# Product-key experts: activations of key rows 48 to 111 made between the gates, and kept in DRAM until they are used

## The chip, the cores and the metric

The program runs on one core of a Trainium2 chip. The core has five engines with queues of their own: TensorE (PE, the matmuls), VectorE (DVE), ScalarE (ACT), GpSimd (POOL) and SyncE (SP, which here only issues DMAs). Each takes its instructions strictly in the order of its queue; semaphores order work between them. The metric is the time of one run on the device in microseconds (us), as the median of three runs.

## The reference

The program computes three transformer layers for 256 tokens with 1024 channels. The change touches the last step alone, a feed-forward layer of 128 x 128 = 16384 experts that are found by product keys:

```
q = (xc @ peer_wq)                     # 8 heads, two half queries each
s = einsum(q, peer_keys)               # scores against 2 x 128 keys
sv, si = top_k(s, 16)                  # best 16 of each half
top_s, pos = top_k(sum of all pairs, 16)
gate = softmax(top_s)                  # 16 experts for each head and token
act = gelu(einsum(peer_u[eidx], xc))
out = einsum(gate * act, peer_v[eidx])
```

Expert (i, c) has the first key i, from here on called its key row (0 to 127), and the second key c (0 to 127).

## The kernel before

The kernel computes the layer densely: gelu(u h) for all 16384 experts, times a gate that is zero wherever an expert was not chosen, times v. Everything stands with 128 partitions (the second key c) by 256 tokens for each key row. The function `peer` has three stages, and the function `peer_route` runs beside the first.

1. **Routing and the first activations.** For each of 8 heads `peer_route` makes the queries and scores on PE, and the best 16 on DVE, then yields; after each yield `peer` makes the activations of two pairs of key rows (`up`, L1939 to L1947). `up` for one pair loads two blocks of u of 512 KB (`wpair`, L448), splits each in two halves of 128x512 into a high part (a cast on ACT, L439) and a low part (a subtraction, L440), runs 2 x 8 x 3 = 48 matmuls (L415 to L417), and takes the gelu on ACT (L1947). In this stage the subtractions go to POOL. Rows 0 to 63 (32 pairs) are made here and stay in SBUF in `act`. The end of the routing turns the chosen keys and gates into `idx`, one transpose for each 128 tokens (`rt`, L2083, L2084).
2. **Gates.** The 64 groups of four tokens each get a gate matrix. `hots` makes one-hot matrices from `idx`: five of each six groups by one comparison on DVE (L1969) and four scalings on ACT (L1977), the sixth by eight comparisons on POOL (L1974, L1975), issued ahead of the other five. `gate` multiplies them on PE (L1983; each of the four products counts as two matmuls in the profile) into one PSUM bank `G` of four. Then DVE multiplies the bank's part for rows 0 to 63 into `act` (L1987), and ACT copies rows 64 to 119 to `Gate` (L1988) and rows 120 to 127 over `x` (L1989).
3. **Second product.** For each pair of rows, `gated` gives the gated activations, split into high and low, and 2 x 8 x 3 = 48 matmuls add v's product into four PSUM banks `acc`. For rows 64 to 127 `gated` first calls `up`, now with the subtractions on DVE, and multiplies by the gate (L2006). The weights of u and v share three load buffers and four split buffers (`weights5`, `weights5h`). At the end DVE adds the residual (L2020) and SP stores it (L2021).

The order of the instructions on each engine is fixed when the program is built: a scheduler moves instructions of different stages past each other where the dependences and buffers allow it (four of the 64 gate products stand among the last activations of stage 1, for one). The chip then runs each queue as it stands.

Of the kernel before, what the change touches and what calls it, by code (L numbers as in the profile page):

```python
# [8 lines left out]
F32, F32R = mybir.dt.float32, mybir.dt.float32r  # L9
# [5 lines left out]
PSUM, DRAM = bass.MemoryType.PSUM, bass.MemoryType.DRAM  # L15

T = 256
D = 1024
KT = 8
# [217 lines left out]
class Ring:  # L237
# [5 lines left out]
    def next(self, shape):  # L243
        self.i += 1
        p = self.pairs[self.i % len(self.pairs)]
        return Pair(*(t.rearrange("p (a b) -> p a b", b=shape[-1]) for t in (p.hi, p.lo)))


class K:
# [1673 lines left out]
    def peer(self):  # L1923

        nc, tc, A, mod = self.nc, self.tc, self.A, self.mod
        v_ = nc.vector
        m2 = mod[:, 96:144]
        sc = self.modscale("norm2_g_2", m2[:, 32:40], "sc6")
        HF = 64
        with ExitStack() as c:  # L1930
            p = c.enter_context(tc.tile_pool(name="pe", bufs=1))
            self.banks(c, a=4, u=2, r=2)

            xd = c.enter_context(tc.tile_pool(name="xwait", bufs=1, space=DRAM)).tile([128, KT, T], F32, name="xd")
            h = self.pair(p, [128, KT, T], "h6")
            self.scaled(self.x, self.r2, sc, m2[:, 24:32], h)
            idx = p.tile([128, 3, T], F32, name="idx")
            iota = p.tile([128, 128], F32, name="iota")
            act = p.tile([128, HF, T], F32, name="acts")  # L1939

            def up(i, out, eng=None):

                self.bank = "u"
                ps = self.psum("act")
                for j in range(2):
                    self.wT(ps[:, T * j:T * j + T], self.wpair(A["u"][i + j], eng), h)
                nc.scalar.activation(out, ps.rearrange("p (j t) -> p j t", j=2), AF.Gelu_apprx_tanh)  # L1947

            with ExitStack() as c2:
                self.W = c2.enter_context(tc.tile_pool(name="weights4", bufs=4))  # L1950
                self.Wh = c2.enter_context(tc.tile_pool(name="weights4h", bufs=8))
                for hd in self.peer_route(c2, h, idx, iota, xd):
                    for i in range(4 * hd, 4 * hd + 4, 2):
                        up(i, act[:, i:i + 2], nc.gpsimd)
                for i in range(32, HF, 2):
                    up(i, act[:, i:i + 2], nc.gpsimd)
            gp = c.enter_context(tc.tile_pool(name="peg", bufs=1))

            G = [gp.tile([128, 120 - HF, T], F32, name="Gate"), self.x]
            self.W = c.enter_context(tc.tile_pool(name="weights5", bufs=3))  # L1960
            self.Wh = c.enter_context(tc.tile_pool(name="weights5h", bufs=4))
            with ExitStack() as c2:
                tp = c2.enter_context(tc.tile_pool(name="pet", bufs=3))
                self.bank = "a"

                def hots(t4, pool):
                    o = tp.tile([128, 2, 4, 128], F32, tag="op" if pool else "o", name=f"oh{t4}", bufs=2 if pool else 3)
                    if not pool:
                        v_.tensor_tensor(o, iota.rearrange("p (a b i) -> p a b i", a=1, b=1).to_broadcast([128, 2, 4, 128]),  # L1969
                                         idx[:, 0:2, 4 * t4:4 * t4 + 4].rearrange("p a (t o) -> p a t o", o=1).to_broadcast([128, 2, 4, 128]), op=OP.is_equal)  # L1970
                    for t in range(4):
                        i1, i2, w = (idx[:, n, 4 * t4 + t:4 * t4 + t + 1] for n in range(3))
                        if pool:
                            nc.gpsimd.tensor_scalar(o[:, 0, t], iota, i1, w, op0=OP.is_equal, op1=OP.mult)  # L1974
                            nc.gpsimd.tensor_scalar(o[:, 1, t], iota, i2, None, op0=OP.is_equal)  # L1975
                        else:
                            nc.scalar.activation(o[:, 0, t], o[:, 0, t], AF.Copy, scale=w)  # L1977
                    return o

                def gate(t4, o):  # L1980
                    ps = self.psum("G")
                    for t in range(4):
                        nc.tensor.matmul(ps[:, 128 * t:128 * t + 128], o[:, 1, t], o[:, 0, t], start=True, stop=True)  # L1983
                    pv = ps.rearrange("p (t i) -> p t i", t=4)
                    ts = slice(4 * t4, 4 * t4 + 4)
                    av = act[:, :, ts].rearrange("p i t -> p t i")
                    v_.tensor_mul(av, av, pv[:, :, :HF])  # L1987
                    nc.scalar.copy(G[0][:, :, ts].rearrange("p i t -> p t i"), pv[:, :, HF:120])  # L1988
                    nc.scalar.copy(G[1][:, :, ts].rearrange("p i t -> p t i"), pv[:, :, 120:])  # L1989

                for g0 in range(0, T // 4, 6):
                    ahead = hots(g0, True)
                    for t4 in range(g0 + 1, min(g0 + 6, T // 4)):
                        gate(t4, hots(t4, False))
                    gate(g0, ahead)
            tp = c.enter_context(tc.tile_pool(name="pea", bufs=2))
            self.bank = "a"
            acc = [self.psum("acc") for _ in range(4)]

            def gated(i):  # L2000
                if i < HF:
                    a = act[:, i:i + 2]
                else:
                    a = tp.tile([128, 2, T], F32, tag="a", name=f"a{i}")
                    up(i, a)
                    v_.tensor_mul(a, a, G[0][:, i - HF:i - HF + 2] if i < 120 else G[1][:, i - 120:i - 118])  # L2006
                return self.split(a, self.pair(tp, [128, 2, T], f"ap{i}", ("ah", "al")))

            nxt = gated(0)
            for i in range(0, 128, 2):  # L2010
                a, nxt = nxt, gated(i + 2) if i < 126 else None
                for j in range(2):
                    vs = self.wpair(A["v"][i + j].rearrange("p (a d) -> p a d", a=2))
                    for m in range(KT):
                        self.mm(acc[m // 2][:, T * (m % 2):T * (m % 2) + T], vs[:, m // 4, 128 * (m % 4):128 * (m % 4) + 128], a[:, j],
                                i + j == 0 and m % 2 == 0, i + j == 127, skip_group_check=True)
            xr = act[:, 0:KT]
            nc.sync.dma_start(xr, xd)
            for m in range(KT):
                v_.scalar_tensor_tensor(xr[:, m], acc[m // 2][:, T * (m % 2):T * (m % 2) + T], m2[:, 40 + m:41 + m], xr[:, m], op0=OP.mult, op1=OP.add)  # L2020
                nc.sync.dma_start(self.out[:, m], xr[:, m])  # L2021
# [133 lines left out]
```

## Time and profile before

| | us |
|---|---|
| runs | 3642.47, 3640.02, 3639.27 (median 3640.02) |
| profiled execution | 3639.1 |
| its span on the core | 3637.3 |
| the last layer's feed-forward, from its first matmuls to the end | about 2711 to 3637.3 |
| gates, from the first product of the dense stretch to the first matmul of the second product | 2977.2 to 3078.8 |

The profile is of one execution. A span is counted from its start, and the start times of instructions count from there too. "Busy" for an engine is the time in which an instruction of its own was being executed; consecutive instructions overlap, so the distance from start to start says how long one occupies the engine, and its duration says when the next engine may go on. The mean granted clock of TensorE over the span was 0.929 of full speed. The median of the runs is 0.9 above the profiled execution, and that is 1.8 above its span.

### The profile page before, as it was taken

To read this page: it belongs to the slowest core of one execution; us is meant where nothing else is said; L and a number is where in the kernel's file an instruction comes from. 1 tells how busy PE (TensorE), PEld (TensorE's weight loads), DVE (VectorE), ACT (ScalarE), POOL (GpSimd) and SP (SyncE) were. 2 spreads that over 40 slices of the span, in tenths; PEclk is the share of its full clock that TensorE was granted. 3 is DMA by queue.
4 is the path that set the end of the run, shared out by engine and by line. 5 is a ranking of instruction groups with operands and counts; after the bars stand their busy time and mean duration, and the time that the engine had idled before them with its cause. 6 is when DMAs were issued, how large, how long until landed. Compare 5 with 4: busy or idle time off the path is not lost.

```text
span 3637.3 us, 69980 instructions
## 1 busy us (share of the span) xinstructions
PE 3312.3 (91%) x27824; PEld 2815.9 (77%) x27824; DVE 2323.3 (64%) x4465; ACT 1691.4 (47%) x3082; POOL 795.0 (22%) x789
## 2 busy tenths in 40 slices
PE   6989889989999999967898989899989887999999
PEld 4769767866678888555777767777879887999999
DVE  3568857754369999367556675666367838555555
ACT  4445332433246666134334344434346568555554
POOL 0000312200000000033232233323338978000000
PEclk9999987989999999978688999889789999999999
DMA  7656573387988999931011111101545330555555
GB/s 286 245 213 225 199 266 101 114 324 320 367 339 339 342 334 339 361 106 39 25 42 37 34 54 44 36 32 58 154 150 178 120 128 18 193 185 182 184 183 165
DMA packets 155276, 641.87 MB, mean 176 GB/s; under 512 B 17192, under 2 KB 36280, under 8 KB 111040
## 3 DMA queue, kind: packets, MB, share of 16 engines
q1 hardware_dynamic: 140736, 563.94, 43.5%
q0 software_dynamic: 14208, 73.41, 5.6%
q8 instruction: 220, 3.60, 0.4%
q14 instruction: 112, 0.92, 0.1%
HBM read 625.87 MB, written 11.40 MB: 175 GB/s over the span
## 4 chain that ended last, share of the span: by engine, by line
PE 40%; DVE 9%; POOL 3%; ACT 2%; issue 1%; DMA 1%; POOLq 0%; SPq 0%; DVEq 0%; ACTq 0%
PE acc L415 3%; PE acc L416 3%; PE acc L417 3%; PE act L417 3%; PE act L415 3%; PE act L416 3%; POOL oh L1974 1%; POOL oh L1975 1%; DVE rs L361 1%; DVE G L1802 1%; PE mc L1682 1%; PE U L1738 1%; PE S L1754 1%; PE R L1732 1%; PE R L1728 1%
## 5 line engine op out<-in xcount | busy, mean ns | idle before, releaser
L1719 POOL MEMSET UV<- 64x256 f32 x64 | 19.5, 306 | 1024.3 <-DVE xT L1169 817.7
L422 PE MATMUL mg<-mg,xs 128*64 128x256 f32 x1408 | 185.0, 386 | 3.7 <-ACT xf L1095 3.7
L1242 ACT ACTIVATE msg<-mg 128x128 f32<-128x128 f32 (+1 forms) x154 | 42.3, 274 | 260.0 <-PE mg L422 190.7
L422 PEld LDWEIGHTS mg<-mg,xs 128*64 128x64 f32 x1408 | 106.2, 138 | 68.1 <-issue 15.8
L361 DVE RECIPROCAL rs<-rs 128x256 f32<-128x256 f32 (+1 forms) x48 | 112.6, 2347 | 53.6 <-ACT rs L360 53.6
L330 PE MATMUL mod<-wm,c 128*32 128x256 f32 x1152 | 98.7, 447 | 51.8 <-DMA wm<-mods 47.3
L327 POOL DMA_DIRECT2D wm<-mods x64 | 34.9, 545 | 390.0 <-PE mod L330 373.4
L330 PEld LDWEIGHTS mod<-wm,c 128*32 128x32 f32 x1152 | 37.5, 121 | 89.3 <-DMA wm<-mods 47.5
L1983 PE MATMUL G<-oh 128*128 128x128 f32 x512 | 80.9, 317 | 25.4 <-ACT oh L1977 12.8
L1983 PEld LDWEIGHTS G<-oh 128*128 128x128 f32 x512 | 74.0, 215 | 31.9 <-ACT oh L1977 17.5
L1243 DVE TENSOR_TENSOR msg<-msg,mg 128x128 f32<-128x128 f32 (+1 forms) x154 | 43.4, 282 | 76.4 <-ACT msg L1242 76.0
L1738 PE MATMUL U<-R,TT 64*64 64x64 f32 x512 | 51.0, 247 | 39.1 <-DVE R L1733 30.9
L1969 DVE TENSOR_TENSOR oh<-iota,idx 128x1024 f32<-128x1024 f32 x53 | 76.1, 1440 | 10.0 <-PE G L1983 10.0
L1987 DVE TENSOR_TENSOR acts<-acts,G 128x256 f32<-128x256 f32 x64 | 44.8, 716 | 58.9 <-ACT acts L1947 49.8
L1738 PEld LDWEIGHTS U<-R,TT 64*64 64x64 f32 x512 | 40.7, 154 | 51.2 <-DVE R L1733 34.2
L1977 ACT ACTIVATE oh<-oh,idx 128x128 f32<-128x128 f32 x212 | 68.1, 392 | 14.2 <-DVE oh L1969 13.9
L1739 ACT ACTIVATE UV<-U 64x256 f32<-64x256 f32 x64 | 24.1, 377 | 102.4 <-PE U L1738 102.2
L1761 DVE TENSOR_TENSOR S<-S,S 128x256 f32<-128x256 f32 x48 | 20.3, 422 | 76.5 <-PE S L1754 76.2
L1974 POOL TENSOR_SCALAR oh<-iota,idx 128x128 f32<-128x128 f32 x44 | 63.6, 1444 | 12.5 <-PE G L1983 12.5
L1146 DVE COPY mgt<-mg 128x128 f32<-128x128 f32 x44 | 12.8, 290 | 74.7 <-PE mg L1139 74.4
L1733 DVE COPY R<-R 64x256 f32<-64x256 f32 x64 | 26.5, 413 | 51.3 <-PE R L1732 50.7
L1802 DVE TENSOR_TENSOR G<-G,X 128x1 f32<-128x1 f32 (+14 forms) x120 | 57.1, 476 | 3.3
(11874 smaller groups left out, 13577.6 us busy)
## 6 DMA issues: line engine op xcount, KB each, us to landing
mg<-m_gu SPq DMA_DIRECT2D x176, 1024.0 KB, 7.5
md<-m_dn SPq DMA_DIRECT2D x88, 1024.0 KB, 7.7
wm<-mods POOLq DMA_DIRECT2D x64, 1024.0 KB, 5.7
w<-u SPq DMA_DIRECT2D x128, 512.0 KB, 3.4
w<-v SPq DMA_DIRECT2D x128, 512.0 KB, 3.3
w<-w_in SPq DMA_DIRECT2D x132, 256.0 KB, 2.6
w<-e_gu SPq DMA_DIRECT2D x44, 512.0 KB, 4.4
w<-e_in SPq DMA_DIRECT2D x24, 512.0 KB, 4.2
```

The lines of the kernel that those rows point to most:

```text
L330: nc.tensor.matmul(ps[32 * j:32 * j + 32, :256], c[:, 2 * kp + k, :], ws[:, 2 * j + k, :], start=kp + k == 0, stop=kp + k == 4)
L361: nc.vector.reciprocal(t[:, :n], t[:, :n])
L415: mm(ps, w.hi, h.hi, start=start, stop=False, **kw)
L416: mm(ps, w.hi, h.lo, start=False, stop=False, **kw)
L417: mm(ps, w.lo, h.hi, start=False, stop=stop, **kw)
L422: mm(ps, w, h, start=start, stop=stop, **kw)
L1738: nc.tensor.matmul(ps[:64, c0_:c0_ + 64], TT[hb, d, o, c], R[hb, d, o], start=True, stop=True)
L1802: v_.tensor_mul(pr[:, :t, :t], G[:, t:t + 1, :t].to_broadcast([128, t, t]), X[:, :t, :t].rearrange("p u s -> p s u"))
L1969: v_.tensor_tensor(o, iota.rearrange("p (a b i) -> p a b i", a=1, b=1).to_broadcast([128, 2, 4, 128]), idx[:, 0:2, 4 * t4:4 * t4 + 4].rear ...
L1974: nc.gpsimd.tensor_scalar(o[:, 0, t], iota, i1, w, op0=OP.is_equal, op1=OP.mult)
L1977: nc.scalar.activation(o[:, 0, t], o[:, 0, t], AF.Copy, scale=w)
L1983: nc.tensor.matmul(ps[:, 128 * t:128 * t + 128], o[:, 1, t], o[:, 0, t], start=True, stop=True)
```

## The change

The rows that are made ahead of the gates are cut from 64 to 48. Rows 48 to 111 (32 pairs) are made in the gates' stage, one `up` after each second gate, with the subtractions on DVE; their gelu goes to a buffer of its own (`as`, two of them), and SP stores it to DRAM (`ad`, 256 KB a pair). In the second product these 32 pairs are loaded back into `a` (three buffers in place of two) ahead of their multiplication by the gate. Rows 112 to 127 (8 pairs) are made there as before. `Gate` grows from 56 to 72 rows, `act` shrinks from 64 to 48, and POOL's one-hot buffer is one in place of two.

```diff
-        HF = 64
+        HF, HD = 48, 112
...
+            ad = [dr.tile([128, 2, T], F32, name=f"ad{i}") for i in range(HF, HD, 2)]
...
-                    o = tp.tile([128, 2, 4, 128], F32, tag="op" if pool else "o", name=f"oh{t4}", bufs=2 if pool else 3)
+                    o = tp.tile([128, 2, 4, 128], F32, tag="op" if pool else "o", name=f"oh{t4}", bufs=1 if pool else 3)
...
                 def gate(t4, o):
+                    self.bank = "a"
                     ps = self.psum("G")
...
+                def spill(i):
+                    a = tp.tile([128, 2, T], F32, tag="as", name=f"as{i}", bufs=2)
+                    up(i, a)
+                    nc.sync.dma_start(ad[(i - HF) // 2], a)
+
+                rows = iter(range(HF, HD, 2))
+                n = 0
                 for g0 in range(0, T // 4, 6):
                     ahead = hots(g0, True)
-                    for t4 in range(g0 + 1, min(g0 + 6, T // 4)):
-                        gate(t4, hots(t4, False))
-                    gate(g0, ahead)
+                    for t4 in (*range(g0 + 1, min(g0 + 6, T // 4)), g0):
+                        gate(t4, ahead if t4 == g0 else hots(t4, False))
+                        n += 1
+                        if n * (HD - HF) // 2 // (T // 4) > (n - 1) * (HD - HF) // 2 // (T // 4):
+                            spill(next(rows))
...
                 else:
-                    a = tp.tile([128, 2, T], F32, tag="a", name=f"a{i}")
-                    up(i, a)
+                    a = tp.tile([128, 2, T], F32, tag="a", name=f"a{i}", bufs=3)
+                    if i < HD:
+                        nc.sync.dma_start(a, ad[(i - HF) // 2])
+                    else:
+                        up(i, a)
                     v_.tensor_mul(a, a, G[0][:, i - HF:i - HF + 2] if i < 120 else G[1][:, i - 120:i - 118])
```

How the queues change is shown at three places. First, POOL's queue where the routing ends, before the change (`w...l` is the low part of a block of u, `oh` a one-hot matrix):

```order
L440 TENSOR_TENSOR w26660l<-w_30176,w26660h 128x512
...
L1974 TENSOR_SCALAR oh_30962<-iota,idx 128x128
L1975 TENSOR_SCALAR oh_30962<-iota,idx 128x128
L1974 TENSOR_SCALAR oh_31049<-iota,idx 128x128
L1975 TENSOR_SCALAR oh_31049<-iota,idx 128x128
L1974 TENSOR_SCALAR oh_31049<-iota,idx 128x128
L1975 TENSOR_SCALAR oh_31049<-iota,idx 128x128
L440 TENSOR_TENSOR w26664l<-w_30176,w26664h 128x512
L1974 TENSOR_SCALAR oh_31049<-iota,idx 128x128
L1975 TENSOR_SCALAR oh_31049<-iota,idx 128x128
L440 TENSOR_TENSOR w26670l<-w_30210,w26670h 128x512
```

and the same place after it:

```order
L440 TENSOR_TENSOR w26660l<-w_30208,w26660h 128x512
...
L1977 TENSOR_SCALAR oh_30434<-iota,idx 128x128
L1978 TENSOR_SCALAR oh_30434<-iota,idx 128x128
L440 TENSOR_TENSOR w26664l<-w_30208,w26664h 128x512
L440 TENSOR_TENSOR w26670l<-w_30242,w26670h 128x512
L440 TENSOR_TENSOR w26674l<-w_30242,w26674h 128x512
L440 TENSOR_TENSOR w26690l<-w_30278,w26690h 128x512
```

With one one-hot buffer in place of two, 8 comparisons stand ahead of w26664l where 12 stood, and none between the subtractions that follow.

Second, ACT's queue amid the gates, before:

```order
L1988 COPY Gate<-G_31353 128x4x56
L1989 COPY xT<-G_31353 128x4x8
L1977 ACTIVATE oh_31406<-oh_31406,idx 128x128 x4
L1988 COPY Gate<-G_31367 128x4x56
L1989 COPY xT<-G_31367 128x4x8
L1977 ACTIVATE oh_31420<-oh_31420,idx 128x128 x4
```

and after, one cycle of two gates and one pair of rows (`as` is the pair's gelu, `w...h` the casts of the next pair's weights):

```order
L1950 ACTIVATE as_30665<-act_30666 128x512
L1992 COPY Gate<-G_30752 128x4x72
L1993 COPY xT<-G_30752 128x4x8
L1980 ACTIVATE oh_30860<-oh_30860,idx 128x128 x4
L439 CAST w26970h<-w_30876 128x512
L1992 COPY Gate<-G_30766 128x4x72
L1993 COPY xT<-G_30766 128x4x8
L1980 ACTIVATE oh_30946<-oh_30946,idx 128x128 x2
L439 CAST w26974h<-w_30876 128x512
L1980 ACTIVATE oh_30946<-oh_30946,idx 128x128 x2
L439 CAST w26980h<-w_30910 128x512
```

A fourth cast and the next gelu follow. On PE each two gates' products now stand between the 48 matmuls of one pair and those of the next, where before the products stood one behind the other.

Third, SP's queue in the second product, where before only loads of v and u stood, after the change (`a` is a pair of activations that comes back from `ad`):

```order
L456 DMA w_35492<-v 128x1024
L2019 DMA a_35560<-ad_27466 128x512
L456 DMA w_35526<-v 128x1024
L456 DMA w_35567<-v 128x1024
L2019 DMA a_35635<-ad_27467 128x512
L456 DMA w_35601<-v 128x1024
L456 DMA w_35642<-v 128x1024
```

One load of 256 KB stands ahead of each two of 512 KB. In the gates' stage the stores to `ad` stand in the same way, one behind each two loads of u.

## Rows read from the trace of the kernel before

**Rows 1.** Busy time by stage: stretch, length, PE, PEld, DVE, ACT, POOL; PEclk, DMA share, GB/s.
```profile
2713.00:2859.00 146.00, 146.00 (x1223) 145.97 (x1222) 109.45 (x510) 99.47 (x192) 125.50 (x99) 1.00 0.55 180
2859.00:2926.00 67.00, 48.38 (x366) 47.19 (x364) 54.85 (x26) 29.88 (x67) 61.48 (x40) 0.90 0.31 107
...
2977.20:3078.80 101.60, 76.49 (x481) 69.96 (x481) 91.41 (x109) 90.88 (x312) 95.85 (x72) 0.90 0.00 1
3078.80:3631.95 553.15, 553.15 (x4608) 552.96 (x4608) 322.71 (x481) 285.53 (x475) 0.00 (x0) 1.00 0.55 181
```
**Rows 2.** The chain that ended last, from 2700 on, by line.
```profile
by line: PE acc L415 13.1%; PE acc L416 13.1%; PE acc L417 13.0%; PE act L417 11.5%; PE act L415 11.5%; PE act L416 11.5%; POOL oh L1974 5.8%; POOL oh L1975 4.9%; DVE oh L1969 1.7%; PE q L416 1.5%; PE q L417 1.5%; PE q L415 1.4%; issue 1.1%
```
**Rows 3.** Waits from 2855 to 3080: total us, times, longest.
```profile
DVE acts L1987 <- ACT acts L1947: 49.8, 1, 49.8
...
PE G L1983 <- POOL oh L1975: 10.5, 7, 2.4
```
**Rows 4.** Timeline of PE: start, us, engine, line, op, names, idle before and its releaser.
```profile
2905.31 0.58 PE L417 MATMUL act<-h6h,w26664l 128*128 128x256 f32 x1 [10.10 <-POOL w26664l L440]
...
2922.71 0.28 PE L416 MATMUL act<-h6l,w26734h 128*128 128x256 f32 x1
2926.01 0.39 PE L415 MATMUL act<-h6h,w26750h 128*128 128x256 f32 x1 [3.02 <-ACT w26750h L439]
...
3004.25 3.12 PE L1983 MATMUL G<-oh 128*128 128x128 f32 x24 [0.37 <-ACT oh L1977]
```
**Rows 5.** Timeline of POOL, ahead of w26664l and amid the gates.
```profile
2899.98 0.60 POOL L1975 TENSOR_SCALAR oh<-iota,idx 128x128 f32<-128x128 f32 x1
...
2904.00 1.26 POOL L440 TENSOR_TENSOR w26664l<-w,w26664h 128x512 fp32r<-128x512 f32 x1
...
3005.97 1.98 POOL L1974 TENSOR_SCALAR oh<-iota,idx 128x128 f32<-128x128 f32 x1
```
**Rows 6.** Timeline of DVE, amid the gates and where POOL subtracts.
```profile
2912.75 8.82 DVE L1969 TENSOR_TENSOR oh<-iota,idx 128x1024 f32<-128x1024 f32 x1 [9.97 <-PE G L1983]
...
2923.43 0.69 DVE L440 TENSOR_TENSOR w27660l<-w,w27660h 128x512 fp32r<-128x512 f32 x1 [1.86 <-ACT w27660h L439]
2924.04 0.69 DVE L440 TENSOR_TENSOR w27661l<-w,w27661h 128x512 fp32r<-128x512 f32 x1
...
3001.91 0.73 DVE L1987 TENSOR_TENSOR acts<-acts,G 128x256 f32<-128x256 f32 x1
3002.52 1.25 DVE L1969 TENSOR_TENSOR oh<-iota,idx 128x1024 f32<-128x1024 f32 x1
3003.65 0.73 DVE L1987 TENSOR_TENSOR acts<-acts,G 128x256 f32<-128x256 f32 x1
```
**Rows 7.** Timeline of ACT, in stage 1 and amid the gates.
```profile
2924.34 0.62 ACT L439 CAST w27671h<-w 128x512 fp32r<-128x512 f32 x1
2924.86 0.59 ACT L1947 ACTIVATE acts<-act 128x512 f32<-128x512 f32 x1
2925.35 0.61 ACT L439 CAST w26750h<-w 128x512 fp32r<-128x512 f32 x1
...
3002.06 1.28 ACT L1977 ACTIVATE oh<-oh,idx 128x128 f32<-128x128 f32 x4
3003.25 0.53 ACT L1988 COPY Gate<-G 128x224 f32<-128x224 f32 x1
3003.58 0.26 ACT L1989 COPY xT<-G 128x32 f32<-128x32 f32 x1
```
**Rows 8.** Timeline where the second product starts.
```profile
3078.76 0.51 PE L415 MATMUL acc<-ap0h,w27660h 128*128 128x256 f32 x2 [1.85 <-ACT ap0h L439]
```
**Rows 9.** DMA issues from 3100 to 3600, and the densest DMA stretch near, as Rows 1.
```profile
w<-v SPq DMA_DIRECT2D x112, 512.0 KB, 3.3
w<-u SPq DMA_DIRECT2D x62, 512.0 KB, 4.0
...
2930.00:2934.00 4.00, 4.00 (x33) 4.00 (x33) 0.00 (x0) 0.79 (x2) 3.55 (x3) 0.91 0.98 368
```

More of the change, by code (lines that the diff above doesn't have):

```diff
@@ L1932, in peer @@
             self.banks(c, a=4, u=2, r=2)
-            xd = c.enter_context(tc.tile_pool(name="xwait", bufs=1, space=DRAM)).tile([128, KT, T], F32, name="xd")
+            dr = c.enter_context(tc.tile_pool(name="xwait", bufs=1, space=DRAM))
+            xd = dr.tile([128, KT, T], F32, name="xd")
+            ad = [dr.tile([128, 2, T], F32, name=f"ad{i}") for i in range(HF, HD, 2)]
             h = self.pair(p, [128, KT, T], "h6")
```

## The prediction

> **What bounds the kernel now.** I read the busy time by stage first. In the second product PE is busy for all of 553.15 us, at full clock, with 4608 matmuls, 0.1200 us each [rows 1]; DVE and ACT are busy for 58% and 52% there. So this stage lasts as long as its matmuls, and taking a pair of rows out of it takes 48 x 0.1200 = 5.76 us off it. In the gates' stretch (2977.2 to 3078.8) PE is busy for 76.49 of 101.60 us at a clock of 0.90, and DMA carries nothing. The chain that ended last says who holds PE up there: POOL's one-hot comparisons (5.8% + 4.9%) stand on it [rows 2], with DVE and ACT close behind, each about 90% busy. How little of that stretch PE needs is read from its timeline: 24 gate matmuls in a row take 3.12 us with a last one of 0.28, so (3.12 - 0.28) / 23 = 0.123 each, and the 480 of this stretch 59 us [rows 1, 4].
>
> The waits name the third fact: DVE's first multiplication of gates waited 49.8 us for the last gelu of stage 1 [rows 3]. The routing was over by then; the gates stood behind the activations of rows 48 to 63, which came at PE's pace. Before that, PE itself lost 10.10 us to one weight part, w26664l, which POOL made only after twelve comparisons, and 3.02 us to ACT [rows 4, 5].
>
> **What is removed, added and moved.** The number of matmuls stays. 8 pairs leave stage 1 and 24 leave the second product; these 32 go between the gates. What the change can win is PE's idle time and slow clock, no more.
>
> *Stage 1.* Up to the wait for w26664l all queues are the same. POOL now makes 8 comparisons ahead of it, the last of which ended at 2899.98 + 0.60 = 2900.6, so the part comes 3.4 us sooner than at 2904.0 and PE resumes at 2901.9 in place of 2905.31 [rows 4, 5]. From there before went through the last part that both have (w26734): 2922.71, and 10 matmuls more, that is 18.7 us, with one gate's 8 matmuls (1.0 us) among them that now come later: 17.7 us, so the first gate starts at 2901.9 + 17.7 = 2919.6. The 3.02 us wait after it [rows 4] stood at a place where ACT had one-hot scalings to wait for; in the new order it has none, and I count it as gone.
>
> *Gates.* One cycle of two gates and one pair is 16 x 0.123 + 48 x 0.120 = 7.73 us of PE; 32 cycles are 247.4 us. Can the others keep that pace? Occupied time, from start to start: a cast 0.52, a gelu 0.49, four scalings 1.19, the copy to Gate 0.33 for 224 elements and up to 0.42 for 288, the small copy 0.26 [rows 7]; a subtraction 0.61, a comparison 1.13, the multiplication 0.61 for 256 elements, between 0.46 and 0.61 for 192 (I take 0.5) [rows 6]. 53 of the 64 gates use ACT and DVE for their one-hots, 11 use POOL. ACT has 4 x 0.52 + 0.49 + 53/32 x 1.19 + 2 x 0.66 = 5.9 us a cycle, DVE 4 x 0.61 + 2 x 0.5 + 53/32 x 1.13 = 5.3. Both are under 7.73, but each waits for the other, so the loop counts: cast 0.62 to its end, subtraction 0.61, multiplication 0.5, comparison 1.25 to its end, four scalings 1.19, cast 0.52, two copies 0.66, two scalings 0.6, cast 0.52, two scalings 0.6, cast 0.52: 7.6 us. That holds for the 21 cycles with two ACT gates. With one from POOL the loop is 0.62 + 0.61 + 0.5 + 1.25 + 1.19 + 0.66 + 2 x 0.52 = 5.9. The mean is 7.0, and since one-hots and parts are made a cycle ahead of PE, the mean decides: PE sets the pace, with 32 x 0.73 = 23 us to spare. I put 4 us for single waits; the bounds are 0 and what the rivals below take. POOL has 8 comparisons every three cycles (23 us); at the slowest seen, 1.98 each, they take 16 [rows 5], so that one buffer does where two were.
>
> *DMA.* Each cycle loads 1 MB and stores 256 KB, about 170 GB/s; the second product then reads 1.25 MB for 5.76 us of PE, 228 GB/s. Both lie well below the 368 GB/s of one stretch of stage 1 [rows 9]. A store waits in SP's queue for its gelu, with the next loads of u behind it; these are for two cycles later and land in 3.3 to 4.0 us [rows 9], so nothing is late. In the second product the load of a pair waits for a subtraction two pairs back, with loads of v behind it. Three buffers at 2.88 us a row give a round of 8.6 us; a landing of 4.0 and the two splits (1.2 to 2.9) leave 1.7 or more. So 0 there, and at worst the price given below.
>
> *Second product.* It begins behind the last pair's gelu: gelu, cast of ap0 and hand-over are about what PE waited there before, 1.85 us [rows 8]. Then 128 x 24 + 16 x 24 = 3456 matmuls at 0.1200: 414.9 us. From the last matmul's end (3631.95, the end of that stretch) to the end of the span 5.35 us as before.
>
> *Sum.* 2919.6 + 247.4 + 1.85 + 414.9 + 5.35 = 3589.1, and 4 for waits: 3593 of span, against 3637.3. With the 1.8 around the span 3595, against 3639.1 of the same execution; the median of the runs shown is 0.9 above that, within what I can't resolve. **I predict 3595 us, 1.2% faster.** The gain is made of the 42 us of the gates' stretch that PE did not need, the 3.4 + 3.0 us at the end of stage 1, and slow clock behind its waits, less the 4 us of waits and what the cycles' start costs.
>
> **Rivals.**
> 1. *The loop through ACT and DVE sets the pace.* For it: it is only 0.13 us shorter than PE's cycle where both gates are ACT's. If four hand-overs cost 0.3 us more each, the cycles are 8.8 and 7.1, mean 8.2: 32 x 0.5 = 16 us, 3607. Against: waits of PE on ACT amid the gates come from one-hots that had no lead, and now they have a cycle's.
> 2. *POOL and DVE block each other.* For it: a comparison on POOL took 1.98 beside DVE's, against 0.60 for the shorter kind alone [rows 5], and one comparison on DVE took 8.82 while POOL subtracted without a pause, against 1.25 [rows 6]. If each of the 88 POOL comparisons holds DVE up for 0.7 us, that is 1.9 a cycle: 7.0 + 1.9 - 7.73 = 1.2 over, 38 us, 3629. Against: amid the gates DVE's comparisons took 1.25 each beside a POOL that never paused; POOL was the one that waited.
> 3. *Slower, by the same place.* If POOL, once ahead, keeps DVE out for its whole batch of eight, as for that one comparison (8.82 - 1.25 = 7.6 us), the eleven batches cost 83 us, less the 23 to spare: 60 over, 3651. It turns into a loss from some 6.2 us a batch. Against it stands the same row as above, and that POOL's comparisons left DVE gaps while its subtractions did not.
> 4. *The loads of saved activations make v late.* If each of 32 delays PE by 1.4 us, 45 us: 3636, no change. For it: SP's queue is strictly in order, and the row of 4.0 us. Against: the slack above.
>
> The Trainium skill (SBUF — State Buffer, Who interferes with whom) says of rivals 2 and 3 that a DVE instruction with two SBUF inputs contends with a GpSimd instruction that reads SBUF, that whichever is issued first holds the shared ports for its whole length, and that the other is blocked. By that rule the subtractions moved to DVE are exposed to POOL's comparisons, which speaks against the change; the trace agrees with it, with either side as the loser, so I give these two a chance but not the likeliest.
>
> **How the numbers follow.** Chances: forecast 0.70 (own range 3587 to 3602), rival 1 0.12, rival 2 0.08, rival 3 0.05, rival 4 0.05. A measurement of this kernel tells about 0.2%, 7 us, from no change. Faster (below 3632.7): forecast, rival 1 and most of rival 2, 0.88; the same: rival 4 and the rest of rival 2, 0.07; slower: rival 3, 0.05. The range goes from 3586 (no wait at all, and a resume at full clock) to 3622 (rival 1 at its worst and a part of rival 2).
>
> **What would show it.** PE resumes by 2902 and the first gate of the dense stretch starts near 2920. Amid the gates PE is busy for over 95% at a clock of 1.00, with 32 cycles of 7.7 to 7.9 us, and no releaser on PE sums to over 5 us. The second product starts near 3169 and takes 415 us, PE busy throughout. Cycles over 8.1 us with PE waiting for casts would be rival 1, DVE's subtractions over 1 us long rivals 2 and 3, gaps in the second product between pairs 48 and 111 rival 4. A sum of PE's waits above 40 us behind 2900 would make the prediction wrong.

## The result, and the profile after

| | runs | median us | from | to |
|---|---|---|---|---|
| before | 6 | 3639.64 | 3632.09 | 3642.47 |
| changed | 6 | 3579.78 | 3571.26 | 3592.48 |

The ratio is 0.9829, with a 95% interval from 0.9802 to 0.9856: faster by 60 us, where 45 were forecast. The time lies 15.2 us below the forecast and 6.2 below the range's low end. The profiled execution took 3590.44 us, with a span of 3588.7, which is 4.6 below the forecast of 3595. So two things have to be explained: what the terms of the sum got wrong, and why the median of the six runs lies 10.7 below the profiled one among them.

Single executions start the feed-forward layer at different moments, from 2700 to 2720 us over the kernels here. I therefore compare the **stretch** from the first query matmul (`q`, L415) to the end of the span: 3637.3 - 2703.7 = 933.6 us before and 3588.7 - 2708.3 = 880.4 after, 53.2 less.

The busy time by stretch after the change, for [rows 1] (stretch, length, PE, PEld, DVE, ACT, POOL; PEclk, DMA share, GB/s):

```profile
2895.00:2926.00 31.00, 22.11 (x173) 21.73 (x173) 16.35 (x12) 11.55 (x27) 22.22 (x19) 0.89 0.35 119
2926.00:2976.00 50.00, 50.00 (x427) 50.00 (x427) 36.51 (x52) 40.48 (x105) 16.43 (x16) 1.00 0.51 162
...
3076.00:3126.00 50.00, 50.00 (x426) 50.00 (x425) 36.14 (x51) 40.04 (x104) 22.85 (x22) 1.00 0.52 170
...
3208.00:3258.00 50.00, 50.00 (x419) 50.00 (x418) 29.65 (x44) 26.08 (x44) 0.00 (x0) 1.00 0.56 182
```

Amid the gates PE is now busy without a gap at a clock of 1.00. DVE, ACT and POOL, which were about 90% busy each in [rows 1], have 10 to 34 us of 50 to spare, and DMA works at half its time.

The waits from 2890 to 3180, for [rows 3] (engine, line, waited for: total us, times, longest):

```profile
POOL oh L1977 <- PE G L1987: 145.5, 10, 21.7
ACT Gate L1992 <- DVE acts L1991: 20.3, 32, 0.8
...
PE act L417 <- POOL w26664l L440: 7.5, 1, 7.5
```

POOL stood on the chain that ended last in [rows 2]; now it waits 145.5 us for the gates of PE. No G of PE waits for a one-hot at all.

PE's timeline, for [rows 4, 8] (start, us, engine, line, operation, names, idle before and its releaser):

```profile
2904.78 0.58 PE L417 MATMUL act<-h6h,w26664l 128*128 128x256 f32 x1 [7.53 <-POOL w26664l L440]
2921.99 1.73 PE L1987 MATMUL G<-oh 128*128 128x128 f32 x14
...
2997.16 1.95 PE L1987 MATMUL G<-oh 128*128 128x128 f32 x16
3004.70 1.95 PE L1987 MATMUL G<-oh 128*128 128x128 f32 x16
3012.24 1.95 PE L1987 MATMUL G<-oh 128*128 128x128 f32 x16
...
3155.50 1.95 PE L1987 MATMUL G<-oh 128*128 128x128 f32 x16
3167.13 0.80 PE L415 MATMUL acc<-ap0h,w28380h 128*128 128x256 f32 x2 [3.93 <-ACT ap0h L439]
```

From the products of two gates to those of the next two it is 7.54 us each time, without a wait. The only waits of PE left behind 2900 are 7.53 us for w26664l and 3.93 for ap0h, twice the 1.85 of [rows 8]. What ap0h itself waited for stands in ACT's timeline:

```profile
3163.70 0.59 ACT L1950 ACTIVATE as<-act 128x512 f32<-128x512 f32 x1
3166.46 0.62 ACT L439 CAST ap0h<-acts 128x512 fp32r<-128x512 f32 x1 [2.17 <-DMA ad<-as]
```

The last stored pair had to leave SBUF first, since the tiles of the second product lie where `as` lay.

### The profile page after: what moved, and what is told of

Read it like the earlier page. It is cut to its first block, busy times and chain, and to the rows that moved or that the text cites. A ratio compares the mean times of both kernels' runs of the same rounds, so it can differ in the third digit from the quotient of the medians.

```text
span 3588.7 us, 70111 instructions
## 1 busy us (share of the span) xinstructions
PE 3295.6 (92%) x27824; PEld 2804.7 (78%) x27824; DVE 2330.4 (65%) x4505; ACT 1687.4 (47%) x3082; POOL 738.0 (21%) x757
## 4 chain that ended last, share of the span: by engine, by line
PE 44%; DVE 8%; ACT 2%; issue 1%; DMA 1%; POOL 0%; SPq 0%; DVEq 0%; ACTq 0%; POOLq 0%
PE acc L415 3%; PE acc L416 3%; PE acc L417 3%; PE act L417 3%; PE act L416 3%; PE act L415 3%; PE G L1987 2%; DVE rs L361 1%; DVE G L1802 1%; PE mc L1682 1%; PE U L1738 1%; PE S L1754 1%; PE R L1732 1%; PE R L1728 1%; PE p L1842 1%
## 5 line engine op out<-in xcount | busy, mean ns | idle before, releaser
L1977 POOL TENSOR_SCALAR oh<-iota,idx 128x128 f32<-128x128 f32 x44 | 59.2, 1345 | 145.5 <-PE G L1987 145.5
L1972 DVE TENSOR_TENSOR oh<-iota,idx 128x1024 f32<-128x1024 f32 x53 | 67.7, 1280 | 0.0
L1987 PE MATMUL G<-oh 128*128 128x128 f32 x512 | 62.6, 275 | 0.0
L1987 PEld LDWEIGHTS G<-oh 128*128 128x128 f32 x512 | 60.1, 192 | 0.0
L422 PE MATMUL ya<-md,mgt 128*64 128x512 f32 x176 | 55.3, 604 | 4.1 <-DVE mgt L1146 4.1
```

Of the source, the lines that this page charges most:

```text
L422: mm(ps, w, h, start=start, stop=stop, **kw)
```

## The experiments

Times of the stretch rest on one profile each. Where some us more appear without a cause in the edit, the first two experiments show one source of them.

**1 and 2. The changed kernel and the kernel before again**, unedited.

> The changed kernel as it is, profiled and timed again. The forecast was 3595; six runs gave 3571 to 3592 with a median of 3579.8, and the one profiled execution (3590.4) has a feed-forward stretch (first query matmul to the end of the span) of 880.4 us, against 933.6 before. Theory A: the stretch is the same in every execution, 880 within 1.5 us, and the differences between the runs (21 us) arise in the some 2700 us ahead of it, which the change leaves alone; then the profiled time minus 880 scatters and the stretch does not. Rival B: the scatter is in the changed stretch (PE losing or keeping the clock behind its wait for w26664l, the stores to DRAM): in an execution that is 10 us faster the stretch is some 870. Rival C: the change makes the 2700 us ahead faster, so that the start of the stretch lies below 2703.7 more often than in the kernel before.

> The kernel before, profiled again. Theory A: stretch 933.6 within 1.5 us, its start anywhere from 2690 to 2712. Rival C: its start near 2703 and not below 2700, while the changed kernel's lies lower.

Measured: changed 3591.6 us (6 runs, 3581.2 to 3599.1) against 3644.4 before (11 runs, 3627.8 to 3658.7), ratio 0.9853 [0.9823, 0.9882]. The stretch was 886.2 in the repeat and 942.3 in that of before, 5.8 and 8.7 longer than first seen, more than I allowed. In both a wait had appeared in code that the change doesn't touch. PE's waits, the changed kernel and then the one before:

```profile
PE s L2066 <- ACT qT L2061: 2.7, 1, 2.7
```
```profile
PE act L417 <- POOL w26664l L440: 10.8, 1, 10.8
...
PE s L2050 <- ACT qT L2045: 2.7, 1, 2.7
```

It costs more than its 2.7 us. In the repeat PE did 393 matmuls in the 51 us around it, at a clock of 0.97; the same stretch of the first profile has 429:

```profile
2804.00:2855.00 51.00, 48.34 (x393) 48.14 (x392) 35.45 (x181) 33.93 (x68) 40.58 (x32) 0.97 0.46 158
```
```profile
2808.00:2859.00 51.00, 51.00 (x429) 50.98 (x428) 37.22 (x171) 34.94 (x67) 43.75 (x35) 1.00 0.54 174
```

36 matmuls at 0.12 us are 4.3 of the 5.8 us. So one and the same program shows stretches from 880 to 886 us, and this wait is one cause. It is not the whole of it: a third profile of the changed kernel (882.8, below) is 2.4 longer than the first without it, and in experiment 8, where it occurs too, PE gets to w26664l only 1.9 us later than in the first profile, against 4.5 here. Of the 8.7 us in the kernel before, 5.2 arise ahead of w26664l and 2.3 in the second product; what caused the latter stays open.

The stretch was thus not the same in each execution, as theory A had it. But it moves by 6 us, while its start moves by 14 in the three profiles of the changed kernel: 2708.3, 2703.8 and 2717.9. So more of the scatter between executions arises ahead of the layer than in it. In the two profiles of before the start is at 2703.7 and 2699.9: the changed kernel does not get there sooner, which speaks against rival C.

**3. Early gates alone**: 48 rows ahead of the gates, none between them.

```
-        HF, HD = 48, 112
+        HF, HD = 48, 48
```

> One part of the change alone: 48 rows ahead of the gates and nothing between the gates (the other 80 rows in the second product). Theory (PE's idle time is all that counts): the gates start near 2920 on the clock of the before profile and run at POOL's pace as before (9.3 us for six gates, 64 gates about 100 us), then 128 x 24 + 80 x 24 = 4992 matmuls at 0.120: 599 us. The stretch is 933.6 less about 10 (the waits of 3.4 and 3.0 us at the end of stage 1, slow clock): 921 to 927. Rival (the 49.8 us wait of DVE for the last gelu of stage 1 was itself a loss): some 885, as in the changed kernel.

Measured: 3642.5 us once, stretch 932.9: nothing gained, less than I expected. PE's waits and its busy time amid the gates:

```profile
PE G L1987 <- POOL oh L1978: 20.3, 14, 2.1
PE G L1987 <- ACT oh L1980: 7.6, 21, 0.9
PE act L417 <- POOL w26664l L440: 7.5, 1, 7.5
```
```profile
2940.00:3032.00 92.00, 68.82 (x422) 63.45 (x421) 73.78 (x94) 79.81 (x270) 85.58 (x72) 0.85 0.00 1
```

The 2.6 and 3.0 us at the end of stage 1 are indeed gone. But the gates now wait 27.9 us for one-hots, where before they waited 23.3: the 10.5 of [rows 3] for POOL's, and for ACT's scalings

```profile
PE G L1983 <- ACT oh L1977: 12.8, 25, 1.0
```

The granted clock there is 0.85 in place of 0.90. Moving the gates earlier only moves PE's idle time. That the gates come earlier explains no part of the gain.

**4. 64 rows ahead, 48 between**, so only the second half of the change.

```
-        HF, HD = 48, 112
+        HF, HD = 64, 112
```

> The other part alone: 64 rows ahead of the gates as before, rows 64 to 111 (24 pairs) between the gates, 8 pairs in the second product. Theory: with 24 pairs for 64 gates a group of eight gates with three pairs needs 3 x 5.76 + 8 x 0.87 = 24.2 us of PE and about 14 of the one-hot chain's 1.74 us a gate plus 9 of casts on ACT, 23; so PE nearly sets the pace, and the stretch is 880 to 890. Rival (the early start of the gates was the gain): 905 to 920.

Measured: 3588.65 us once, stretch 880.6, against 880.4. 24 pairs spread over the gates cover them as well as 32 do; PE had no wait for a one-hot. Together with 3 this puts the whole gain on the pairs between the gates.

**5. 80 rows between the gates**: all that are left.

```
-        HF, HD = 48, 112
+        HF, HD = 48, 128
```

> The changed kernel with all 80 remaining key rows made between the gates instead of 64 (40 pairs over 64 gates; none is left for the second product). Theory A (work per matmul is the same wherever it stands, once TensorE has no idle time amid the gates): stretch within 3 us of the changed kernel's, no wait for G's one-hots, gates last 18 us x 8/8 = some 40 to 46 us longer (8 more pairs of 48 matmuls of 0.12 us) and the second product is shorter by as much. Rival B (rows between gates are themselves cheaper or dearer than rows in the second product): the stretch moves by 5 us or more.

Measured: 3591.53 us once, stretch 881.1. The gates end 47 us later, just over the 40 to 46 expected, and the second product is as much shorter. Theory A holds: once PE has no idle time, it doesn't matter where a pair is made.

**6. No comparisons of the first group on POOL.**

```
-                    ahead = hots(g0, True)
+                    ahead = hots(g0, True) if g0 else None
...
-                        gate(t4, ahead if t4 == g0 else hots(t4, False))
+                        gate(t4, ahead if ahead and t4 == g0 else hots(t4, False))
```

> The changed kernel, but POOL makes no comparisons for the first group of gates, so nothing stands before the split of the last weight of the score stage (w26664l) on POOL; VectorE and ScalarE make all six of that group. Theory A (TensorE's idle time is all that counts): the 7.5 us wait for w26664l falls under 2 us and the feed-forward stretch (first q matmul to the end, 880.4 us in the changed kernel's profile, up to 886.2 where the scores wait 2.7 us for qT) is 6 to 10 us shorter: 870 to 875, or 876 to 880 with that wait. Rival B (the wait only moves: the first gate waits for VectorE's and ScalarE's one-hots instead): a wait for oh of 5 us or more stands at the first gates, and the stretch is the same within 2 us.

Measured: 3592.0 us once, stretch 880.9, and the wait for w26664l is again 7.5 us. The time is what theory B said, but its wait for one-hots at the first gates did not appear, so both theories missed. POOL's timeline shows why (the same columns as PE's):

```profile
2891.70 2.27 POOL L440 TENSOR_TENSOR w26660l<-w,w26660h 128x512 fp32r<-128x512 f32 x1
2893.97 1.77 POOL L1977 TENSOR_SCALAR oh<-iota,idx 128x128 f32<-128x128 f32 x1
...
2903.29 0.60 POOL L1978 TENSOR_SCALAR oh<-iota,idx 128x128 f32<-128x128 f32 x1
2903.86 1.26 POOL L440 TENSOR_TENSOR w26664l<-w,w26664h 128x512 fp32r<-128x512 f32 x1
```

Eight comparisons still stand there: the ones of the next group took the free place in the queue. The experiment did not remove what it was to remove.

**7. No comparisons on POOL at all**: DVE and ACT make all 64 sets.

```
-                for g0 in range(0, T // 4, 6):
-                    ahead = hots(g0, True)
-                    for t4 in (*range(g0 + 1, min(g0 + 6, T // 4)), g0):
-                        gate(t4, ahead if t4 == g0 else hots(t4, False))
+                if True:
+                    for t4 in range(T // 4):
+                        gate(t4, hots(t4, False))
```

> The changed kernel, except that POOL makes no one-hots for any group: VectorE and ScalarE make all 64 sets, in the order of the tokens (in e5_nopool0 only the first group's were taken from POOL, and eight of the next group's came to stand before the split of w26664l, so the wait stayed at 7.5 us). Theory A (whatever eight comparisons stand ahead of w26664l on POOL, they are the wait): w26664l's wait falls under 2 us, ap0h's stays near 3.9 us, no G waits for one-hots, and the stretch is 870 to 875 us (the changed kernel's 880.4 less 6 to 10), 5.8 us more if the scores wait 2.7 us for qT. Rival B (the saving of e9_all, 12 us, came from its earlier start of the second product alone): stretch 878 to 882.

Measured: 3584.3 us once, stretch 874.6, as theory A had it. PE's resume and the busy time amid the gates:

```profile
2895.55 0.38 PE L417 MATMUL act<-h6h,w26664l 128*128 128x256 f32 x1 [0.53 <-POOL w26664l L440]
```
```profile
2976.00:3026.00 50.00, 50.00 (x426) 50.00 (x426) 40.34 (x55) 41.46 (x112) 0.00 (x0) 1.00 0.52 184
```

The comparisons were the wait for w26664l. And POOL, which set the pace before, isn't needed amid the gates: DVE and ACT do its share and still have 8 us of 50 to spare.

**8. The stored activations' buffers kept apart from the second product's.**

```
+            keep = c.enter_context(tc.tile_pool(name="pek", bufs=1))
...
-                    a = tp.tile([128, 2, T], F32, tag="as", name=f"as{i}", bufs=2)
+                    a = keep.tile([128, 2, T], F32, tag="as", name=f"as{i}", bufs=2)
```

> The changed kernel with the buffers of the spilled activations (as) in a pool that stays open, so that the first split rows of the second product (ap0) do not lie where as lay. Theory A (ap0h waits for the last store of as): the wait of the second product's first matmul for ap0h falls from 3.9 us to 1.7 to 2.2 us, as before the change, and from the last gate matmul to the first matmul of the second product it takes some 2 us less (11.0 us in the changed kernel). Rival B (ap0h waits for the last activation and ScalarE's queue in any case): 3.9 us stays within 0.4 us.

Measured: 3598.0 us once (its layer began 11 us later than in the changed kernel's profile), stretch 876.5 with a wait of 2.6 us for qT in it. PE where the second product starts:

```profile
3168.76 1.95 PE L1988 MATMUL G<-oh 128*128 128x128 f32 x16
3176.30 0.28 PE L415 MATMUL acc<-ap0h,w28380h 128*128 128x256 f32 x1
```

The wait is gone altogether, not only the 2.2 us of the store that theory A had counted: 7.54 us from the last gates to the second product in place of 11.63. ACT's timeline shows why:

```profile
3171.90 0.64 ACT L439 CAST ap0h<-acts 128x512 fp32r<-128x512 f32 x1
...
3176.97 0.59 ACT L1950 ACTIVATE as<-act 128x512 f32<-128x512 f32 x1
```

The cast of ap0h now stands ahead of the last pair's casts and gelu in ACT's queue; in the changed kernel it stood behind that gelu and the store. So the buffer in the same place had cost the store's landing and the place in the queue, and this run does not show how the 3.93 us split between the two, beyond the 2.17 that the trace of the changed kernel puts down to the store.

From there to the end it is 419.9 in place of 421.6. In the changed kernel PE, behind its 3.93 us of idle time, ran the first matmuls at a granted clock of 0.50, the lower of its two levels (1.2 GHz), 0.21 us apart; here the clock is 1.00 from the first one on. The changed kernel, then this run:

```profile
3168.00:3170.00 2.00, 2.00 (x11) 2.00 (x11) 0.41 (x1) 0.00 (x0) 0.00 (x0) 0.50 0.85 299
```
```profile
3176.30:3178.30 2.00, 2.00 (x19) 2.00 (x18) 2.00 (x4) 1.59 (x3) 0.00 (x0) 1.00 0.65 244
```

That is 4.1 + 1.7 = 5.8 us for a wait of 3.9.

**9 and 10. 7 and 8 together, with the first two rows split ahead of the last pair**, and the changed kernel a third time beside its repeat. To the edits of 7 and 8 come:

```
+            ap0 = self.pair(keep, [128, 2, T], "ap0")
...
+                            if n == T // 4:
+                                self.split(act[:, 0:2], ap0)
...
-                    a = tp.tile([128, 2, T], F32, tag="a", name=f"a{i}", bufs=3)
+                    a = keep.tile([128, 2, T], F32, tag="as", name=f"a{i}", bufs=2)
...
-            nxt = gated(0)
+            nxt = ap0
```

> The changed kernel with three edits: POOL makes no one-hots at all (VectorE and ScalarE make all 64 sets, in the order of the tokens), as in a pool that stays open, and the first two rows of the second product are split ahead of the last two spilled activations. Theory A: w26664l's wait of 7.5 us and ap0h's of 3.9 us both go or fall under 1.5 us, no wait in their place, VectorE and ScalarE stay under 50 us of 50 amid the gates (forecast 41 to 44), and the stretch is 9 to 13 us shorter than the changed kernel's 880.4; the time is 0.25 to 0.36 percent below the changed kernel's, ratio to the kernel before 0.981 to 0.983 where the changed kernel's was 0.9853 on this chip. Rival B (VectorE or ScalarE becomes the bound amid the gates): waits of G for oh come back, cycles are over 7.7 us, and the stretch is no shorter than 880.

> The changed kernel again, beside e11_all in the same call, to see how far the median moves from one set of runs to another: 3579.8 in the first six runs, 3591.6 in the next six. Theory A (the first set lay low by scatter): median 3583 to 3595, ratio to the kernel before 0.983 to 0.987. Rival B (the change is worth 60 us and the second set lay high): 3575 to 3582, ratio under 0.983. Theory C on what differs between executions: where the scores wait for qT some 2.7 us, the feed-forward stretch is 885 to 888 us, elsewhere 879 to 882.

> The same kernel as e9_all (no one-hots on POOL, the buffers of the spilled activations kept apart, the first rows of the second product split early), beside the changed kernel in the same call. Theory A: its median is 9 to 13 us below e10_again's, its stretch 866 to 872 us (5.8 more where the scores wait for qT). Rival B (e9_all's lower time was scatter): the medians differ by less than 4 us.

Measured:

| | median us | ratio to before | stretch |
|---|---|---|---|
| changed, second set | 3591.6 | 0.9853 [0.9823, 0.9882] | 886.2 |
| all edits | 3581.0 | 0.9812 [0.9780, 0.9843] | 868.4 |
| changed, third set | 3590.5 | 0.9847 [0.9820, 0.9874] | 882.8 |
| all edits again | 3586.1 | 0.9827 [0.9801, 0.9853] | 874.9 |

In the first profile of all edits, PE goes from its last gates straight to the second product:

```profile
3149.74 1.95 PE L1989 MATMUL G<-oh 128*128 128x128 f32 x16
3157.28 0.28 PE L415 MATMUL acc<-ap0h,w28380h 128*128 128x256 f32 x1
```

Its stretch is 12.0 us shorter than the changed kernel's first: 5.8 by experiment 7 and 5.8 by 8 account for 11.6 of it. From the last gates to the second product it takes the same 7.54 us as in 8, so the early split adds nothing there. In its repeat the scores waited for qT twice, 5.3 us, and the stretch was 6.5 longer. By the profiles this version beats both kernels. The times agree in sign, but their intervals overlap, and the 4.4 us within one set lies between what the two theories said; a gain over the changed kernel is likely, but its size, 4 to 12 us by these figures, is not settled.

The third set of the changed kernel bears out theory A on its median and ratio. Its stretch, 882.8, had no wait for qT and still lay just above the 879 to 882 of theory C; its wait for w26664l was 8.2 us. All 18 runs of the changed kernel have a median of 3590.0 (3571 to 3605), all 39 of the one before 3644.4 (3628 to 3670).

## Why the prediction was right, and where it was wrong

The direction and the mechanism were right. PE's idle time amid the gates was what could be won (experiments 3 to 5), PE set the pace of the gates, and the second product was bound by its matmuls throughout. The size was under-estimated. Measured from the first query matmul, which shifts the forecast's moments by 2703.7 (us):

| step | forecast | after | difference |
|---|---|---|---|
| PE resumes with w26664l | 198.2 | 196.5 | -1.7 |
| from there to the first dense gate | 17.7 | 17.2 | -0.5 |
| 32 cycles | 247.4 | 241.2 | -6.2 |
| single waits | 4.0 | 0 | -4.0 |
| start of the second product | 1.85 | 3.93 | +2.1 |
| second product and end | 420.3 | 421.6 | +1.3 |
| stretch | 889.3 | 880.4 | -8.9 |

(The cycles after are the time from 2921.99 to 3167.13 less the wait of 3.93. The differences add up to -9.0 for rounding.)

- **The step that failed is "One cycle of two gates and one pair is 16 x 0.123 + 48 x 0.120 = 7.73 us".** It is 7.54 us. The pair's 48 matmuls are 0.120 apart as forecast, so the 16 gate matmuls have (7.54 - 5.76) / 16 = 0.111 us each. I had taken 0.123 as the mean of a run of 24 [rows 4]. The clock is not the reason: its stretch had 0.90 in the mean [rows 1], but that run itself had 1.00, the upper level (2.4 GHz), as the gates have after the change. The busy time over the run, and the scalings of its last one-hots:

```profile
3004.25:3007.40 3.15, 3.12 (x24) 2.92 (x24) 3.15 (x5) 3.15 (x12) 3.15 (x3) 1.00 0.01 3
```
```profile
3005.54 1.28 ACT L1977 ACTIVATE oh<-oh,idx 128x128 f32<-128x128 f32 x4
```

  The trace's own start times show what made the mean dear: 19 of the 23 steps from one matmul to the next are 0.111 or 0.112 us already, as after the change. The first step, behind the wait of 0.37 [rows 4], is 0.21. Three near the end are 0.14 to 0.18; there the weights of one product after the other are loaded 0.29 us apart, the pace of these scalings (four in 1.19 us). The price held small waits for one-hots, which the change itself was forecast to end.
- **The 4 us for single waits did not come.** The lead of a cycle was enough for every one-hot and every part; the argument against rival 1 had said as much, and I added the allowance all the same.
- **The start of the second product was priced by a row of before, 1.85 [rows 8], and took 3.93.** What is late in the new kernel is a store that the old one didn't have, by way of a buffer in the same place, and the cast's place in ACT's queue. PE then started at half clock, which makes up the +1.3 of the next step. I had listed the store in SP's queue, but not who takes over its buffer (experiment 8).
- **w26664l** came 5.1 us sooner than before (201.6 to 196.5), where 3.4 were forecast, for the reason given, eight comparisons in place of twelve; it was the 7.5 us left that experiment 7 took away.
- **The low end of the range, 3586,** kept the cycles at 7.73 us, so it covered no mistake in that price. With every step as measured the sum comes to 3595 - 8.9 = 3586, the end itself. It also had nothing for the scatter of executions: the three runs that were shown lie within 3.2 us of each other, while the 39 runs of that kernel lie within 42, up to 31 within one set.
- **What put the time outside the range.** Of the 15.2 us below the forecast, 4.6 are in the profiled execution: its stretch is 8.9 shorter than forecast, but began 4.5 later than in the profile of before (the rest is rounding). The other 10.7 are from that execution to the set's median, and no term of the sum is about them. The first set's median, 3579.8, is 10 us below that of all 18 runs; the second and third set lie inside the range. So it was the scatter that took the first set out of the range, by luck of the draw; the sets inside it do not make the price of the cycle right. Over all runs the change is worth 3644.4 - 3590.0 = 54.4 us in place of 45, which fits the 8.9. Where the scatter comes from is only partly known: the start of the layer moves by up to 20 us over the kernels here, the wait for qT is up to 6 us of it, and among the 33 runs of before whose clock was listed the longer ones have the lower mean granted clock (correlation -0.78; 0.921 at 3669.8 us). What lowers the clock from run to run stays open.

**The rivals.** 1 (the loop through ACT and DVE): no G waited for a one-hot, and the spacing is 7.54 us throughout; refuted. 2 and 3 (POOL and DVE block each other): DVE's comparisons amid the gates took the same with POOL's beside them as without, the changed kernel and then experiment 7 (count, least/median/most ns):

```profile
L1972 DVE TENSOR_TENSOR oh<-iota,idx x49: 1201/1218/1233, 2925.0 to 3142.6; 128x1024 f32<-128x1024 f32 x49
```
```profile
L1972 DVE TENSOR_TENSOR oh<-iota,idx x58: 1202/1218/1230, 2926.0 to 3143.3; 128x1024 f32<-128x1024 f32 x58
```

DVE's subtractions there took 0.67 to 0.81 us, below the 1 us that was to be the sign of these rivals. Amid the gates POOL alone paid. Its comparisons there spread far wider:

```profile
L1977 POOL TENSOR_SCALAR oh<-iota,idx x40: 789/1034/2091, 2938.9 to 3149.1; 128x128 f32<-128x128 f32 x40
```

Of these 40, the ones that ran beside no DVE instruction took 0.79 to 0.80 us, those beside a whole comparison of DVE 1.86 to 2.09. The rule of the Trainium skill (SBUF — State Buffer, Who interferes with whom), that the engine which issues first holds the shared ports and the other is blocked, allows either loser. At the end of stage 1 the loser had been DVE: its subtraction at 2915.18, beside POOL's own, took 2.59 us. Amid the gates the loser was POOL, and it had the time. Rival 4 (saved activations make v late): DVE waited for the loads in the second product, while PE's only wait from 3160 to 3590 was the 3.9 us for ap0h:

```profile
DVE a L2022 <- DMA a<-ad: 19.3, 21, 2.0
```

## What to carry to other kernels

Price an instruction from the steps in which nothing held it up, and look at single start times for that: the mean of a run that holds small waits is too dear for a stage that will have none, even where the clock is the same. When work is added that stores a buffer, ask which tile is laid over that buffer next, since the store's landing becomes a wait there and moves the first writer back in its queue. And before a range is set, take the scatter of the unchanged kernel's executions from more than three runs, or leave room for it.

## What was not expected of the hardware

- A wait of 3.9 us ahead of a dense stretch of matmuls cost 5.8 (experiment 8): behind it they were 0.21 us apart instead of 0.12, at a granted clock of 0.50.
- A batch of eight POOL comparisons took 9.9 us ahead of w26664l in the changed kernel (2893.57 to 2903.46), with single ones between 0.59 and 2.59 us. Where POOL is the one that gives way, the cheapest move was to take its share away: 38 to 43 us of 50 for DVE and ACT, and 5.8 us less in all.
